# A WKV recurrence on one core: zeros and some thirty steps of the first twelve pairs get other places in the written-out order

## The chip, the cores and the metric

The kernel runs on one core of a Trainium2 chip. The metric is device time in microseconds (us), the median of several executions. The core's engines each work through their own queue in order: PE (TensorE, matmul) with its weight loads, DVE (VectorE), ACT (ScalarE), POOL (GpSimd) and SP (SyncE, which only issues transfers here). They meet through semaphores. Sixteen DMA engines move the data.

## The reference

For each batch and each channel a state (aa, bb) is carried over 2048 time steps, with a running maximum pp for numerical safety. `k` and `v` are 16 x 2048 x 256 in float32, `w` and `u` are vectors of 256.

```python
for t in range(seq_len):
    ww = u + k[b, t];  qq = np.maximum(pp, ww)
    e1, e2 = np.exp(pp - qq), np.exp(ww - qq)
    output[b, t] = (e1 * aa + e2 * v[b, t]) / (e1 * bb + e2 + 1e-08)
    ww = pp - w + k[b, t];  qq = np.maximum(ww, k[b, t])
    e1, e2 = np.exp(ww - qq), np.exp(k[b, t] - qq)
    aa, bb, pp = e1 * aa + e2 * v[b, t], e1 * bb + e2, qq
```

So every output is a ratio of two exponentially weighted sums over the past, with an extra weight `u` on the present step.

## The kernel before

Time is cut into 16 chunks of 128 steps (c = 0 to 15), batches into groups of four, so there are 64 work items, `n` = 0 to 63, which the text calls pairs; chunk c holds pairs 4c to 4c + 3. Each loads 512 KB of `k` and as much of `v`. A program lists the steps of all pairs, gives each a place (a number), sorts them, and emits them in that order as far as their conditions and free buffers allow; each engine then executes its own steps in the order in which they were emitted. The steps that matter here:

- `LK n`, `LV n`: the loads, issued by POOL from pair 3 on (L108, L111, L115). `RK n`: `k` rounded to the matmul type (L194; DVE, or POOL for n = 11, 15, 19 and so on; pairs 3 to 10 are loaded in the rounded type's tile and need none). `CV n`: `v` cast to bf16 (L214; DVE for n under 10, POOL from 10 on).
- `R q n` and `L q n` (q = 0, 1): PE builds the exponents of half q of pair n in an X tile of PSUM (L201, four small matmuls, and L207, two large ones). There are two X tiles. `X q n`: ACT takes the exp of them into the ring EZR (L210), which frees the tile.
- `TV n`: DVE multiplies these weights by `v` (L219). `S n`: PE sums them over time into TOT (L246).
- The state of chunk c, when its four S are done: `CS` (DVE copies the sums, L252), `TU` (PE turns them, L259), `SL` (ACT, logarithm, L263), `FR` and `OF` (DVE, frames by a scan, and offsets, L268 to L276), `SN` (DVE, one value for the next chunk, L279), `SW` (ACT, exp, L282), `CH` (DVE, the chain by two scans, L286 to L289), `SS` (DVE, L296), `KP` (DVE, L299), `TK` (PE turns the result back into the PSUM tile TURN, L303), `BK` (DVE copies TURN out, L307).
- The output of pair n: `DEN n` (PE, twelve matmuls into an X tile, L323), `LN n` and `INV n` (ACT: exp of minus the logarithm gives the reciprocal, L335, L340), `NUM n` (PE, twelve matmuls, L323), `MUL n` (DVE, L355), `ST n` (the stores, SP). Pair n's output comes ten pairs behind its input.

Ahead of some of PE's steps stand zero matmuls (L149): products of a zero tile, written to TURN, that nothing reads. They keep PE at work while it would wait. Their numbers come from the table `Z0` for chunk or pair 0 and `Z` for the rest. From `TK` to `BK` none are emitted, since TURN holds a result then (`quiet`). Places come from the table P; the dictionary `AT` overrides single ones:

```python
key = name if isinstance(name, str) else " ".join(map(str, name))
ops[name] = dict(place=AT.get(key, place), fn=fn, args=args, after=list(after), take=take, give=give, mode=mode)
```

Of the kernel before, what the change touches and what calls it, by code (L numbers as in the profile page):

```python
# [15 lines left out]
def kernel(  # L16
# [37 lines left out]
    FILL = 1  # L54
# [4 lines left out]
         "R": [-0.795, -7.965],  # L59
         "OUT": {"DEN": [-0.47, -0.155, -0.55, -0.495], "LN": [-11.935, -9.86, -0.84, -6.17], "INV": [-13.87, -8.32, -4.99, -5.82], "NUM": [-0.105, 0.155, 0.11, -5.15], "MUL": [1.115, 0.345, 0.895, 1.035], "ST": [-5.05, 7.26, 1.245, 7.765], "SQ": [-3.365, 6.69, -2.4, 8.84]},  # L60
         "TAIL": {"DEN": -4.36, "LN": -16.54, "INV": 3.8, "NUM": -0.31, "MUL": 4.39, "ST": 14.35, "step": 2.989, "SQ": 26.08},
         "Z0": {"L": 1, "S": 3, "DEN": 0, "NUM": 6, "TK": 47, "TU": 17, "R": 12},
         "Z": {"DEN": 0, "L": 1, "NUM": 0, "TK": 4, "S": 0, "TU": 1, "R": 0}}

    AT = {"INV 55": 69.0, "SL 15": 69.1, "LN 56": 69.2, "SW 15": 75.7, "FR 15": 69.3}

    consts = ctx.enter_context(tc.tile_pool(name="consts", bufs=1))
    kpool = ctx.enter_context(tc.tile_pool(name="kpool", bufs=NK))
# [63 lines left out]
    Z = consts.tile([128, 192], BF16, tag="Z", name="Z")  # L132
# [14 lines left out]
    def zeros(m, first=False):  # L147
        for j in range(m):
            K(PE.matmul(TURN[:, 0:192], Z[:, 0:128], Z, start=first, stop=True, skip_group_check=True))  # L149
# [72 lines left out]
    AS, D1, L1, A0, FR, BC, A2 = range(7)  # L222
# [88 lines left out]
    RD, NUM, OT = {}, {}, {}  # L311
# [66 lines left out]
    def step(name, place, fn, args=(), after=(), take=None, give=(), mode=0):  # L378
        key = name if isinstance(name, str) else " ".join(map(str, name))
        ops[name] = dict(place=AT.get(key, place), fn=fn, args=args, after=list(after), take=take, give=give, mode=mode)  # L380

# [51 lines left out]
    while todo:  # L433
        for name in todo:
            o = ops[name]
            if all(x not in ops or "done" in ops[x] for x in o["after"]) and (xs if o["take"] == "X" else free.get(o["take"], 1)):
                break
        else:
            raise AssertionError(todo[:9])
        todo.remove(name)  # L440
        args = list(o["args"])
        if o["take"] == "X":
            held[name] = xs.pop(0)
            args.append(held[name])
        elif o["take"]:
            free[o["take"]] -= 1
        elif name[0] == "L":
            args.append(held[("R",) + name[1:]])
        for g in o["give"]:
            if g == "X":  # L450
                x = held[("DEN", name[1]) if name[0] == "LN" else ("NUM", name[1]) if name[0] == "MUL" else ("R",) + name[1:]]
                xs.append(x)
                args.append(x)
            else:
                free[g] += 1
        if o["mode"] and not quiet:
            zeros(P["Z0" if name[-1] < FILL else "Z"].get(name[0], 0))
        quiet = quiet and name[0] != "BK" or name[0] == "TK"
        o["fn"](*args)
        o["done"] = True  # L460
# [30 lines left out]
```

## Time and profile before

| | |
|---|---|
| Median of three runs | 289.46 us (288.67 to 289.91) |
| The profiled execution | 289.2 us on the device, span 287.5 us |
| Busy in the span | PE 271.6 us (94%, zeros included), ACT 258.6 (90%), DVE 246.9 (86%), POOL 176.4 (61%) |
| Moved | 101.20 MB, 352 GB/s on the mean |
| ACT idle ahead of pair 8's exps | 4.38 us, ended by L207 of PE |
| The zeros ahead of TK 0 | 47, 4.05 us from 29.07 us on |

Times in the profile count from the start of the span; the device time also holds what lies around it. A timeline row gives start and length in us, engine, line of the kernel, operation, output and inputs, how many instructions are merged in the row, and in brackets the idle time of the engine ahead of it and what ended it. A step such as `X 0 8` is not named in the profile: it is the seventeenth instruction of L210.

### The profile page before, as it was taken

What the parts mean: (1) busy time and instruction counts of PE and PEld (TensorE: products, weight loads), DVE (VectorE), ACT (ScalarE), POOL (GpSimd) and SP (SyncE); (2) the same over time, 40 slices, a digit from 0 to 9 for tenths busy, and PEclk for the clock granted to TensorE, in tenths of its full rate; (3) what the DMA queues carried; (4) which work ended last, traced back from release to release, by engine and by line L of the source; (5) the groups of instructions that cost most, each with busy time, mean ns of one, the idle gap of its engine ahead of it and who ended that gap; (6) DMA issues with size and microseconds to landing.
All of it is one profiled execution on the core that took longest, in us unless ns stands there. A gap on an engine that the chain in (4) does not pass through costs nothing.

```text
span 287.5 us, 8058 instructions
## 1 busy us (share of the span) xinstructions
PE 271.6 (94%) x3263; PEld 139.2 (48%) x3263; DVE 246.9 (86%) x422; ACT 258.6 (90%) x291; POOL 176.4 (61%) x219
## 2 busy tenths in 40 slices
PE   7989999999999999999999999999999999998860
PEld 6535744454545545454545545454545545454530
DVE  4685879989897979989898989989898989889861
ACT  1776399999999999999999999999999999998991
POOL 8256458575767687575767687575767685421320
PEclk9999999999999999999999999999999999999997
DMA  6999999999999999999999999999999999985896
GB/s 206 348 354 346 347 348 313 384 369 390 374 394 381 383 393 372 391 382 393 355 392 388 389 387 382 394 385 395 370 380 374 389 394 387 347 237 177 235 278 179
DMA packets 58669, 101.20 MB, mean 352 GB/s; under 512 B 5152, under 2 KB 43688, under 8 KB 58632
## 3 DMA queue, kind: packets, MB, share of 16 engines
q0 software_dynamic: 21200, 65.42, 65.5%
q1 hardware_dynamic: 37280, 35.14, 36.4%
q8 instruction: 25, 0.41, 0.6%
q10 hardware_dynamic: 152, 0.14, 0.1%
q14 instruction: 12, 0.10, 0.1%
HBM read 67.12 MB, written 33.55 MB: 350 GB/s over the span
## 4 chain that ended last, share of the span: by engine, by line
PE 81%; ACT 6%; DMA 4%; DVE 4%; issue 2%; SPq 1%; DVEq 0%; ACTq 0%
PE X L207 20%; PE X L323 15%; PE num L323 12%; PE X L201 12%; PE TURN L149 11%; PE TOT L246 7%; DMA ot<-in_v_dram 4%; ACT rd L335 3%; PE TOT L259 2%; DVE ot L355 2%; ACT rd L340 2%; DVE EZR L219 1%; ACT EZR L210 1%; PE TURN L303 1%; SPq L115 1%
## 5 line engine op out<-in xcount | busy, mean ns | idle before, releaser
L210 ACT ACTIVATE EZR<-X 128x1024 bf16<-128x1024 f32 x128 | 126.9, 1014 | 14.4 <-PE X L207 14.2
L214 POOL CAST vb<-vr 128x1024 bf16<-128x1024 f32 x54 | 56.4, 1044 | 69.3 <-DVE EZR L219 67.5
L219 DVE TENSOR_TENSOR EZR<-EZR,vb 128x2048 bf16<-128x2048 bf16 x64 | 77.8, 1219 | 0.4 <-ACT EZR L210 0.2
L355 DVE TENSOR_TENSOR ot<-num,rd 128x1024 f32<-128x1024 f32 x60 | 73.3, 1221 | 3.9 <-ACT rd L340 3.6
L340 ACT ACTIVATE rd<-rd 128x1024 f32<-128x1024 f32 (+1 forms) x65 | 68.0, 1046 | 2.0
L335 ACT ACTIVATE rd<-X 128x1024 f32<-128x1024 f32 (+1 forms) x65 | 65.8, 1012 | 2.3 <-PE X L323 0.7
L149 PE MATMUL TURN<-Z 128*128 128x192 bf16 x319 | 55.2, 259 | 1.4 <-DVE Z L133 1.4
L201 PE MATMUL X<-WU,CO 64*64 64x512 bf16 x512 | 51.9, 390 | 0.9 <-DVE WU L176 0.6
L149 PEld LDWEIGHTS <-Z 128*128 128x128 bf16 x319 | 28.4, 100 | 48.6 <-issue 47.1
L115 POOL DMA_DIRECT2D vr<-in_v_dram x61 | 46.3, 759 | 6.7 <-DVE vb L214 5.9
L207 PE MATMUL X<-kr,NLE 128*128 128x512 f32 x128 | 45.6, 438 | 0.0
L207 PE MATMUL X<-kr,NLZ 128*128 128x512 f32 x128 | 45.5, 437 | 0.0
L108 POOL DMA_DIRECT2D kf<-in_k_dram x53 | 40.1, 756 | 0.0
L194 DVE CAST kr<-kf 128x1024 fp32r<-128x1024 f32 x39 | 31.6, 839 | 4.0 <-DMA kf<-in_k_dram 4.0
L201 PEld LDWEIGHTS <-CO 64*64 64x64 bf16 x512 | 15.7, 105 | 31.1 <-issue 26.3
L323 PE MATMUL X<-EZR,S 64*64 64x512 bf16 x256 | 26.2, 394 | 1.7 <-ACT rd L335 1.0
L323 PE MATMUL X<-cb,Id 64*64 64x512 bf16 x256 | 25.9, 376 | 0.0
L323 PE MATMUL X<-EZR,Id 64*64 64x512 bf16 x256 | 25.9, 376 | 0.0
L323 PE MATMUL num<-EZR,SN 64*64 64x512 bf16 x240 | 24.3, 386 | 1.1 <-DVE ot L355 1.1
L246 PE MATMUL TOT<-EZR,OH 128*32 128x256 bf16 x512 | 23.7, 277 | 1.3 <-DVE EZR L219 1.3
L323 PE MATMUL num<-cb,IdN 64*64 64x512 bf16 x240 | 24.0, 376 | 0.0
L323 PE MATMUL num<-EZR,IdN 64*64 64x512 bf16 x240 | 23.9, 376 | 0.0
(69 smaller groups left out, 269.3 us busy)
## 6 DMA issues: line engine op xcount, KB each, us to landing
vr<-in_v_dram POOLq DMA_DIRECT2D x61, 512.0 KB, 7.7
kf<-in_k_dram POOLq DMA_DIRECT2D x53, 512.0 KB, 8.5
out_dram<-ot SPq DMA_DIRECT2D x64, 256.0 KB, 10.0
out_dram<-ot SPq DMA_DIRECT2D x116, 128.0 KB, 10.1
kr<-in_k_dram POOLq DMA_DIRECT2D x8, 512.0 KB, 8.8
ot<-in_k_dram SPq DMA_DIRECT2D x3, 512.0 KB, 5.9
ot<-in_v_dram SPq DMA_DIRECT2D x3, 512.0 KB, 10.0
out_dram<-ot POOLq DMA_DIRECT2D x11, 128.0 KB, 3.4
```

Source lines behind the costliest of these rows:

```text
L115: K((SP if n < BYSP else POOL).dma_start(out=vr, in_=rows_of(v, n)))
L149: K(PE.matmul(TURN[:, 0:192], Z[:, 0:128], Z, start=first, stop=True, skip_group_check=True))
L201: K(PE.matmul(X[a][o:o + HS, i, :].rearrange("p (n d) -> p n d", n=2), CO[r:r + HS, q, :], WU[r:r + HS, :].unsqueeze(1).broadcast_to([HS, ...
L207: K(PE.matmul(X[a][:, i, :], (NLE, NLZ)[q], km[:, i, :], start=False, stop=True, skip_group_check=True))
L210: K(SC.activation(ez(n)[:, q, 1], X[a], ACT.Exp))
L214: K((DVE if n < EARLY else POOL).tensor_copy(vb, VR.pop(n)))
L219: K(DVE.tensor_mul(ez(n)[:, :, 0], ez(n)[:, :, 1], vb.unsqueeze(1).broadcast_to([128, 2, 2, D])))
L246: K(PE.matmul(t[32 * j:32 * j + 32, 0:256], OH[:, s:s + 32], ez(n)[:, 0, 1 - q, i, 256 * x:256 * x + 256], start=p == 0 and x == 0, stop=p ...
L323: K(PE.matmul(out_tile[o:o + HS, i, :], left, right, start=s == 0, stop=s == 2, tile_position=(r, o), skip_group_check=True))
L335: K(SC.activation(RD[n][:, i], X[a][:, i], ACT.Ln, scale=RS))
L340: K(SC.activation(RD[n][:, i], RD[n][:, i], ACT.Exp, scale=-1.0))
L355: K(DVE.tensor_mul(o.rearrange("p (i n) d -> p i (n d)", i=2)[:, i], NUM[n][:, i], RD[n][:, i]))
```

## The change

Two things. The numbers of zeros in `Z0` fall (`TK` 47 to 8, `TU` 17 to 2, `R` 12 to 6; the last goes for both halves of pair 0), and a new dictionary `ZAT` puts four zeros each ahead of TU 1, DEN 0 and R 0 11, where none were. And thirty entries of `AT` give steps of pairs 0 to 11 and of the states of chunks 0 and 1 new places.

```diff
-         "Z0": {"L": 1, "S": 3, "DEN": 0, "NUM": 6, "TK": 47, "TU": 17, "R": 12},
+         "Z0": {"L": 1, "S": 3, "DEN": 0, "NUM": 6, "TK": 8, "TU": 2, "R": 6},
...
-    AT = {"INV 55": 69.0, "SL 15": 69.1, "LN 56": 69.2, "SW 15": 75.7, "FR 15": 69.3}
+    AT = {"INV 55": 69.0, "SL 15": 69.1, "LN 56": 69.2, "SW 15": 75.7, "FR 15": 69.3, "TU 0": 5.01, "FR 0": 5.02,
+          "SW 0": 6.2, "TK 0": 7.205, "CV 7": 6.4, "TV 5": 5.1, "S 4": 5.3, "S 5": 7.195, "TV 6": 6.3,
+          "S 6": 7.21, "S 7": 8.1, "CH 0": 6.32, "SS 0": 6.33, "BK 0": 7.21, "CV 6": 5.2, "TV 7": 7.3,
+          "KP 0": 8.6, "TV 8": 8, "R 0 6": 5.0, "R 0 8": 7.19, "R 0 9": 7.9, "CS 1": 8.2, "TU 1": 8.3,
+          "SN 0": 8.15, "FR 1": 8.95, "CV 9": 8.0, "SW 1": 9.6, "RK 11": 9.1}
+
+    ZAT = {"DEN 0": 4, "TU 1": 4, "R 0 11": 4}
...
-            zeros(P["Z0" if name[-1] < FILL else "Z"].get(name[0], 0))
+            zeros(ZAT.get(" ".join(map(str, name)), P["Z0" if name[-1] < FILL else "Z"].get(name[0], 0)))
```

Sorted by these places, with their conditions, the queues come out as follows (zeros in brackets; up to CV 5 on DVE, X 1 5 on ACT and L 1 6 on PE the order is the same, and behind the last step shown too):

```text
PE before   TU 0[17] R 0 7 L 0 7[1] R 1 7 L 1 7[1] TK 0[47] S 4 S 5 R 0 8 L 0 8 R 1 8 L 1 8 S 6
            R 0 9 L 0 9 R 1 9 L 1 9 S 7 R 0 10 L 0 10 R 1 10 L 1 10 TU 1 DEN 0 NUM 0[6]
            R 0 11 L 0 11[1] R 1 11 L 1 11[1]
PE after    TU 0[2] S 4 R 0 7 L 0 7[1] R 1 7 L 1 7[1] R 0 8 L 0 8[1] R 1 8 L 1 8[1] S 5 TK 0[8] S 6
            R 0 9 L 0 9[1] R 1 9 L 1 9[1] S 7 TU 1[4] R 0 10 L 0 10[1] R 1 10 L 1 10[1] DEN 0[4] NUM 0[6]
            R 0 11[4] L 0 11[1] R 1 11 L 1 11[1]
DVE before  CV 6 FR 0 OF 0 CH 0 SS 0 KP 0 TV 5 CV 7 TV 6 TV 7 SN 0 CV 8 TV 8 CV 9 CS 1 BK 0 RK 12 FR 1 OF 1 SN 1
DVE after   FR 0 OF 0 TV 5 CV 6 TV 6 CH 0 SS 0 CV 7 BK 0 TV 7 SN 0 CS 1 KP 0 CV 8 TV 8 CV 9 FR 1 OF 1 SN 1 RK 12
ACT before  X 0 6 X 1 6 SL 0 X 0 7 X 1 7 SW 0 X 0 8 X 1 8 X 0 9 X 1 9 X 0 10 X 1 10 SL 1 LN 0 INV 0 X 0 11 SW 1 X 1 11
ACT after   X 0 6 SL 0 X 1 6 SW 0 X 0 7 X 1 7 X 0 8 X 1 8 X 0 9 X 1 9 SL 1 X 0 10 X 1 10 LN 0 INV 0 SW 1 X 0 11 X 1 11
POOL before CV 10 RK 11          POOL after  RK 11 CV 10          (loads in the same order in both)
```

## The prediction, made before the changed kernel was run

> **What bounds the kernel now.** I read the page first, then busy time by stretch, then the ACT, PE and DVE timelines from 24 to 50 us, and last each load's issue and landing in the trace.
>
> From the page, engine totals, the granted clock and the exps:
>
> ```profile
> PE 271.6 (94%) x3263; PEld 139.2 (48%) x3263; DVE 246.9 (86%) x422; ACT 258.6 (90%) x291; POOL 176.4 (61%) x219
> PEclk9999999999999999999999999999999999999997
> L210 ACT ACTIVATE EZR<-X 128x1024 bf16<-128x1024 f32 x128 | 126.9, 1014 | 14.4 <-PE X L207 14.2
> ```
>
> Busy time by stretch (length; PE, PEld, DVE, ACT, POOL; clock; DMA share; GB/s):
>
> ```profile
> 28.80:36.00 7.20, 7.20 (x89) 5.38 (x87) 6.29 (x14) 2.81 (x5) 2.99 (x4) 1.00 1.34 348
> 36.00:43.00 7.00, 7.00 (x78) 3.44 (x70) 5.38 (x11) 6.34 (x8) 4.03 (x5) 1.00 1.02 348
> 100.00:200.00 100.00, 99.83 (x1222) 49.17 (x1220) 92.50 (x148) 98.51 (x111) 70.20 (x80) 1.00 1.05 385
> ```
>
> PE's high share says little, since zero matmuls fill its waits. ACT works 98.51 of 100 us in the long middle, where four pairs take 16.18 us each time (the first exp of pairs 26, 30, 34 starts at 105.10, 121.28, 137.46). So the middle is bound by ACT, and a change before it counts by how much sooner ACT's unbroken run begins. That is at about 46 us:
>
> ```profile
> 27.23 0.28 ACT L263 ACTIVATE U<-TOT 128x128 f32<-128x128 f32 x1 [0.84 <-PE TOT L259]
> 28.25 2.04 ACT L210 ACTIVATE EZR<-X 128x1024 bf16<-128x1024 f32 x2 [0.74 <-PE X L207]
> 30.19 0.36 ACT L282 ACTIVATE G<-U 128x192 f32<-128x192 f32 x1
> 34.94 2.02 ACT L210 ACTIVATE EZR<-X 128x1024 bf16<-128x1024 f32 x2 [4.38 <-PE X L207]
> ...
> 46.42 1.03 ACT L335 ACTIVATE rd<-X 128x1024 f32<-128x1024 f32 x1 [0.16 <-PE X L323]
> ```
>
> The largest hole is 4.38 us ahead of pair 8's exps, which wait for PE. What PE does there (start, length):
>
> ```profile
> 25.17 1.58 PE L149 MATMUL TURN<-Z 128*128 128x192 bf16 x17
> 26.58 0.61 PE L259 MATMUL TOT<-Sel,ts 128*128 128x96 f32 x4
> ...
> 29.07 4.05 PE L149 MATMUL TURN<-Z 128*128 128x192 bf16 x47
> 32.96 0.39 PE L303 MATMUL TURN<-Id,CB 128*128 128x128 bf16 x4
> 33.28 0.62 PE L246 MATMUL TOT<-EZR,OH 128*32 128x256 bf16 x16
> 33.83 0.41 PE L201 MATMUL X<-WU,CO 64*64 64x512 bf16 x4
> ```
>
> TK 0, with its 47 zeros, stands ahead of pair 8's rows and logs. Loads are the other limit: until 46 us they land one after another every 1.5 us (k8 29.05, k9 32.0, k10 35.1, k11 38.09, v10 39.59, k12 41.13, v11 42.62), as 512 KB at 350 GB/s does. No reordering brings them sooner.
>
> **Zeros at the very start.** R 0 0 and R 1 0 get 6 zeros instead of 12. The first six are hidden: PE waits for WU until 6.83 anyway. The second six (0.08 us each) bring the exps of pairs 0 to 3 some 0.3 to 0.5 us forward, and this ends at v2: it lands at 16.16, CV 2 and then TV 1 (16.86) and S 1 (18.13) wait for it, and R 0 4 stands behind S 1. Worth 0.
>
> **Zeros at TU 0 and SL 0's place.** 15 zeros go, 15 x 0.083 = 1.24 us (the 47 took 3.9 us), so TU 0 starts at 25.34 instead of 26.58 and SL 0 runs from 25.99 (0.65 after TU, as before) to 26.27. SL 0 now stands ahead of X 1 6, which so starts 0.91 us later than before, at 26.27. S 4 comes behind TU 0 (TV 4 ended at 25.80), 0.33 us.
>
> **FR and OF ahead of CV 6, SW 0 ahead of X 0 7.** DVE ends CV 5 at 26.41, the frames and offsets take 1.23 us (28.65 to 29.88), so SW 0 starts at 27.69 and holds ACT for 0.26 us (44.98 to 45.24). X 0 7 follows at 27.95 (before 28.25), X 1 7 at 28.97. The late X 1 6 costs nothing, since ACT waits for SW 0.
>
> **TK 0 behind pair 8.** Steps from the rows of before: exp end to the next rows in its X half 0.20, rows to logs 0.36 to 0.38, logs to the next PE step 0.64, logs to exp 0.75, an exp 1.02. R 0 8 at 29.17, L 0 8 at 29.55 (k8 landed at 29.05), X 0 8 at 30.30 instead of 34.94, 4.64 us sooner; X 1 8 at 31.32. The rest of the walk is where this gain is spent.
> S 5 starts at 31.21 and TK 0's 8 zeros at 31.54 end at 32.20. On DVE, TV 5, CV 6 and TV 6 now stand ahead of CH 0 (1.22 + 0.69 + 1.22 behind 27.64), and CH 0 with SS 0 takes 1.30, to 32.05: the zeros hide this wait, and without them it would be 0.5 us. TK 0 0.40, S 6 0.33, R 0 9 at 32.93. A new wait: the zero ahead of L 0 9 writes TURN, which BK 0 reads. BK 0 stands behind CV 7 on DVE (32.74) and takes 0.68, to 33.42; L 0 9, and all of PE behind it, starts at 33.54, about 0.2 late. X 0 9 at 34.29 (37.27), 2.98 sooner. R 1 9 34.18, L 1 9 34.56, S 7 at 35.20.
> CS 1 ends 1.0 us after S 7's start (38.16 to 39.16 before), at 36.20, and **TU 1**, which now stands ahead of pair 10, waits for it; its 4 zeros lie inside this wait, and R 0 10, both logs of 10 and DEN 0 stand behind it. TU 1 36.24, R 0 10 36.78, L 0 10 37.16, X 0 10 37.91 (39.61), 1.70 sooner. L 1 10 38.18, then DEN 0's 4 zeros, 0.33 us in the open (it also waits for X 0 10's end at 38.93), DEN 0 39.15, LN 0 0.89 later at 40.04 (41.81). NUM 0 with its 6 zeros as before (0.77 + 0.60 + 0.67), then R 0 11's 4 new zeros, 0.33 in the open: R 0 11 at 41.52, X 0 11 at 42.65 (44.06), 1.41 sooner. L 1 11 42.92, S 8 and S 9 at 43.56 (0.55), DEN 1 44.11 (45.53), LN 1 at 45.00 (46.42): 1.42 sooner. From here the order is that of before, and ACT has no holes.
>
> **RK 11, RK 12 and the loads.** RK 11 can start when k11 lands (38.09) and ends at 39.13, not at 41.74; L 0 11 at 41.90 would just be served either way, so this hides under PE. CV 10 then runs at v10's landing, as before, and LK 14, LV 13 and LK 15 go out about 1.1 us sooner, behind a queue that is full to 45.5 us. LV 10 and LK 12, behind the later CV 6, go out 0.5 us later, in a queue of 10 us: nothing. RK 12 now stands behind FR 1, OF 1 and SN 1 and ahead of TV 9. DVE reaches it at 40.4, k12 lands at 41.13, the cast takes 0.7 to 1.14 us, TV 9 ends at 43.1 to 43.5, and S 9 needs it at 43.84: 0.3 us to spare.
>
> **Sum.** 1.4 us, which with roundings of 0.02 to 0.04 us at some ten links is 1.4 to 1.5. In the profiled execution's terms 289.2 - 1.45 = 287.75; its 289.2 lies 0.26 under the median of the runs, so I put the same gain on the median: 289.46 - 1.45 = 288.0. That is 0.5%, about what a measurement of this kernel can tell from no change, so half of this case lies on either side of that bound. The unknown is the price of the 12 new zeros between other steps: nothing (a zero ahead of logs costs 0.02: rows to rows is 1.02 us with it, 1.00 without), or 0.083 each, 1.0 in all. I take the latter, by the 47. Its own range is 287.4 to 288.6.
>
> **Rival: more is kept.** If the zeros cost nothing (1.0 us less) and BK 0 is out of the way (0.2), X 0 9's lead of 2.98 shrinks only to about 2.6: 286.8. For it: PE bubbles hide single zeros. Against: the long rows give 0.083 each. Chance 0.22.
>
> **Rival: the loads take it back.** In the middle k arrives just in time; DVE waits for it at 88, 104 and 185 us:
>
> ```profile
> 88.31 0.70 DVE L194 CAST kr<-kf 128x1024 fp32r<-128x1024 f32 x1 [0.61 <-DMA kf<-in_k_dram]
> 104.56 0.69 DVE L194 CAST kr<-kf 128x1024 fp32r<-128x1024 f32 x1 [0.67 <-DMA kf<-in_k_dram]
> ```
>
> With ACT 1.45 us sooner, loads that can't come sooner hold DVE for that much more each fourth pair; about 0.5 us of it is free (MUL 3 ends at 57.9, NUM 4 follows at 58.4), so some 0.95 of the gain goes: 289.0. Against: the DMA dips to 254 to 340 GB/s from 43 to 50 us and moves 400 at its best against 385 on the mean, so it can catch up before 88 us; and the 0.6 us waits leave ACT's 16.18 us untouched. Chance 0.13.
>
> **Rival on the slow side: PE's rate falls.** 66 zeros go and 18 come (12 by name, 6 ahead of the logs of pairs 8 to 10, which no longer lie between TK 0 and BK 0). Of the first 38, the last 15 took 1.40 us (0.093 each) and the first 23 3.42 (0.149), though the clock column says 1.00: PE starts slow and speeds up after 3.4 us, by 1.6. If PE's waits in the walk (0.3 us at 27.2, 0.7 at 28.5, and 1.2 at 5.6 from the halved zeros of the start) were enough to bring the slow rate back, the stretch from 31.2 to 44.1, in which PE has 12 us of work, would grow by 0.6 for each us so spent. It decides above 4.8 us of such work (2.9 us lost against the forecast); all of it costs 7.2 us. I price it in the middle, 4.5 us lost: 292.5. Against: from 270 to 278 us PE is busy 1.49 of each 2.00 us and the four-matmul groups still follow each other in 0.21 us. Chance 0.10. The Trainium skill, TensorE: Matmul & The Clock Gate, Part 1, says that the clock halves after an idle window of about 3.4 us and returns after a busy one; the start agrees with the 3.4 us, and by that rule waits of 0.7 us keep full rate, but fewer zeros speak against the change as soon as they add up within a window.
>
> That nothing happens is no rival: the list of steps, sorted by the new places, differs on every engine.
>
> **How the numbers follow.** Forecast 0.55, more kept 0.22, loads 0.13, PE's rate 0.10. Faster by over 0.5%: half of the forecast (0.28) and nearly all of the second (0.21), with rounding 0.50. Within: the other half, the loads and a little over, 0.38. Slower: the last, and a worse case of the loads, 0.12. The range runs from 286.6, the second case with 0.2 us to spare, to 289.8, no gain and the spread of the runs.
>
> **What would show it.** Right: X 0 8 at 30.3, X 0 9 at 34.3, X 0 10 at 37.9, LN 1 at 45.0, and from there 1.4 us sooner throughout, to pair 63's exps (254.76 before). Wrong: a hole other than those at 28, 32 to 34 and 37 us; L 0 9 not held by BK 0; RK 12 holding TV 9; DVE waits for k over 1 us after 50 us with ACT holes behind them; matmul groups at more than 0.21 us spacing.

## The result, and the profile after

The changed kernel takes 288.46 us (median of 14 runs, 286.87 to 288.83) beside 289.39 us for the kernel before (14 runs, 288.60 to 290.06). The ratio of the two is 0.995, interval 0.9936 to 0.9964: about 1.45 us at 289.39, between 1.04 and 1.85 by the interval (it compares runs made beside each other; the two medians lie 0.93 apart). The forecast was 288.0 with a gain of 1.45. The profiled execution took 288.83 us with a span of 287.1 (before 289.2 and 287.5). Lines of the changed kernel stand six lower than before: L207 is now L213, L210 is L216, and so on. (The new entries of `AT` are 28, not thirty.)

The page of the changed kernel: totals, the granted clock in 40 slices, and the exps' group.

```profile
PE 268.5 (94%) x3215; PEld 134.8 (47%) x3215; DVE 248.5 (87%) x422; ACT 259.0 (90%) x291; POOL 175.7 (61%) x219
PEclk9999999999999999999999999999999999999996
L216 ACT ACTIVATE EZR<-X 128x1024 bf16<-128x1024 f32 x128 | 126.8, 1014 | 11.5 <-PE X L213 11.5
```

The clock holds in every slice but the last, as before. The exps' waits for PE fell from 14.2 us to 11.5, but the span fell by only 0.4, so not all that the exps won arrived at the end. The ACT timeline of the changed kernel, first the stretch that the change reorders (28 to 47 us), then two lines much later:

```profile
27.64 1.92 ACT L216 ACTIVATE EZR<-X 128x1024 bf16<-128x1024 f32 x2
29.83 2.04 ACT L216 ACTIVATE EZR<-X 128x1024 bf16<-128x1024 f32 x2 [0.27 <-PE X L213]
33.69 2.05 ACT L216 ACTIVATE EZR<-X 128x1024 bf16<-128x1024 f32 x2 [1.82 <-PE X L213]
37.29 2.04 ACT L216 ACTIVATE EZR<-X 128x1024 bf16<-128x1024 f32 x2 [0.74 <-PE X L213]
42.25 2.04 ACT L216 ACTIVATE EZR<-X 128x1024 bf16<-128x1024 f32 x2 [0.43 <-PE X L213]
44.61 1.02 ACT L341 ACTIVATE rd<-X 128x1024 f32<-128x1024 f32 x1 [0.31 <-PE X L329]
...
140.08 1.02 ACT L216 ACTIVATE EZR<-X 128x1024 bf16<-128x1024 f32 x1 [0.35 <-PE X L213]
142.44 1.02 ACT L341 ACTIVATE rd<-X 128x1024 f32<-128x1024 f32 x1 [0.15 <-PE X L329]
```

The single hole of 4.38 us ahead of pair 8 is gone; smaller ones of 0.27, 1.82 and 0.74 us stand ahead of pairs 8, 9 and 10. LN 1 starts at 44.61 where it was 46.42, so the front of the kernel is 1.81 us ahead of the profiled execution of before (part of this is that execution's late start, as shown below). The last two lines are new: ACT, which had no wait for PE there before, now waits at pair 35's exps and once more behind them. The first exp of each pair, in us:

| | before | forecast | after | sooner by |
|---|---|---|---|---|
| X 0 7 | 28.25 | 27.95 | 27.64 | 0.61 |
| X 0 8 | 34.94 | 30.30 | 29.83 | 5.11 |
| X 0 9 | 37.27 | 34.29 | 33.69 | 3.58 |
| X 0 10 | 39.61 | 37.91 | 37.29 | 2.32 |
| X 0 11 | 44.06 | 42.65 | 42.25 | 1.81 |
| LN 1 | 46.42 | 45.00 | 44.61 | 1.81 |
| X 0 12 | 48.44 | | 46.63 | 1.81 |
| pair 36 | | 1.4 sooner | | 1.08 |
| pair 63 | 254.76 | 1.4 sooner | 253.98 | 0.78 |

The lead is 1.81 us at pair 12 and stays so to pair 34. It loses 0.73 at pairs 35 and 36, and 0.33 at pair 56. Another 0.41 goes behind pair 63: the last MUL ends 27.12 us after X 0 63 in both executions, but from there to the end of the span, in which the last stores land, it takes 6.01 us instead of 5.60. That leaves the 0.37 us by which the span fell. PE's timeline of the changed kernel where the spread zeros and the new wait lie:

```profile
31.07 0.83 PE L155 MATMUL TURN<-Z 128*128 128x192 bf16 x8
31.75 0.39 PE L309 MATMUL TURN<-Id,CB 128*128 128x128 bf16 x4
32.06 0.40 PE L252 MATMUL TOT<-EZR,OH 128*32 128x256 bf16 x8
32.40 0.41 PE L207 MATMUL X<-WU,CO 64*64 64x512 bf16 x4
32.91 0.24 PE L155 MATMUL TURN<-Z 128*128 128x192 bf16 x1
32.94 0.71 PE L213 MATMUL X<-kr,NLE 128*128 128x512 f32 x2
```

TK 0's eight zeros, TK 0, S 6, R 0 9, then the single zero ahead of L 0 9. It starts 0.51 us after R 0 9, where such a zero follows its rows by 0.34 to 0.35 elsewhere, because BK 0 reads TURN on DVE until 32.86:

```profile
32.17 0.69 DVE L313 CAST cb<-TURN 128x512 bf16<-128x512 f32 x1 [0.32 <-PE TURN L309]
```

The new wait is where the forecast put it, though BK 0 itself waited 0.32 us for TK 0 and not for CV 7.

Where the lead goes is in three lines of the changed kernel, DVE first, then PE:

```profile
136.13 0.99 DVE L200 CAST kr<-kf 128x1024 fp32r<-128x1024 f32 x1 [1.70 <-DMA kf<-in_k_dram]
137.04 1.21 DVE L361 TENSOR_TENSOR ot<-num,rd 128x1024 f32<-128x1024 f32 x1
138.30 0.41 PE L329 MATMUL num<-EZR,SN 64*64 64x512 bf16 x4 [0.76 <-DVE ot L361]
```

DVE reaches RK 36 early and stands still for 1.70 us until k36 lands at 136.10; in the kernel before it landed at 136.06. A MUL queued behind it starts that much later, the next NUM on PE waits 0.76 us for the tile that MUL frees, and ACT's two holes at 139.7 and 142.3 follow.

### The profile page after: what moved, and what is told of

It is laid out like the page before. It is cut to its first block, busy times and chain, and to the rows that moved or that the text cites. A ratio compares the mean times of both kernels' runs of the same rounds, so it can differ in the third digit from the quotient of the medians.

```text
span 287.1 us, 7961 instructions
## 1 busy us (share of the span) xinstructions
PE 268.5 (94%) x3215; PEld 134.8 (47%) x3215; DVE 248.5 (87%) x422; ACT 259.0 (90%) x291; POOL 175.7 (61%) x219
## 4 chain that ended last, share of the span: by engine, by line
PE 53%; DMA 23%; ACT 10%; DVE 8%; issue 3%; SPq 0%; POOL 0%; DVEq 0%; ACTq 0%; POOLq 0%
DMA out_dram<-ot 19%; PE X L213 14%; PE X L329 10%; PE num L329 8%; PE X L207 8%; PE TURN L155 7%; PE TOT L252 4%; ACT rd L341 4%; ACT EZR L216 3%; DVE ot L361 3%; DMA kr<-in_k_dram 3%; ACT rd L346 2%; DMA WUf<-in_u_dram 2%; DVE EZR L225 2%; PE TOT L265 1%
## 5 line engine op out<-in xcount | busy, mean ns | idle before, releaser
L216 ACT ACTIVATE EZR<-X 128x1024 bf16<-128x1024 f32 x128 | 126.8, 1014 | 11.5 <-PE X L213 11.5
L155 PE MATMUL TURN<-Z 128*128 128x192 bf16 x271 | 53.0, 262 | 1.5 <-DVE Z L139 1.4
L207 PE MATMUL X<-WU,CO 64*64 64x512 bf16 x512 | 51.9, 390 | 1.7 <-DVE WU L182 1.0
L155 PEld LDWEIGHTS <-Z 128*128 128x128 bf16 x271 | 24.5, 101 | 50.6 <-issue 49.1
L213 PE MATMUL X<-kr,NLE 128*128 128x512 f32 x128 | 45.6, 437 | 0.7 <-DMA kr<-in_k_dram 0.7
L213 PE MATMUL X<-kr,NLZ 128*128 128x512 f32 x128 | 45.5, 436 | 0.0
L207 PEld LDWEIGHTS <-CO 64*64 64x64 bf16 x512 | 15.8, 104 | 32.2 <-issue 27.2
```

Of the source, the lines that this page charges most:

```text
L207: K(PE.matmul(X[a][o:o + HS, i, :].rearrange("p (n d) -> p n d", n=2), CO[r:r + HS, q, :], WU[r:r + HS, :].unsqueeze(1).broadcast_to([HS, ...
L213: K(PE.matmul(X[a][:, i, :], (NLE, NLZ)[q], km[:, i, :], start=False, stop=True, skip_group_check=True))
L216: K(SC.activation(ez(n)[:, q, 1], X[a], ACT.Exp))
```

## Experiments

The questions: does the order, or the number of zeros, bring the gain; what do the twelve new zeros cost; does the start matter; and is it the loads that take part of it back? Times are medians; each ratio is to the kernel before, run beside it.

**The zeros alone.** The kernel before, with the three numbers of the change and its old order.

```diff
-"TK": 47, "TU": 17, "R": 12
+"TK": 8, "TU": 2, "R": 6
```

> The order of before with the smaller numbers of zeros (TK 8, TU 2, R 6) and none of the four new places. Theory A (the walk: both the zeros and the order are needed, since DVE and the loads stand behind the zeros): TU 0 1.2 us sooner, but FR 0 stays behind CV 6, which waits for v6; TK 0 starts when SS 0 is done, about 31.7 instead of 32.96; S 5 then waits for TV 5, so pair 8's first exp is 0.3 to 0.6 us sooner (34.4 against 34.94), and RK 12 at k12's landing (41.1) holds FR 1 and TV 9 as before, so LN 1 is at most 0.3 us sooner than 46.42. Time 289.1, ratio 0.998 to 1.000. Rival (the zeros alone are the change, the order adds little): LN 1 1.2 us sooner or more, ratio 0.996 or below.

Measured: 291.05 us, ratio 1.0049 (1.0027 to 1.0071): slower, which neither theory allowed. From its PE timeline, and its busy time by stretch (length; PE, PEld, DVE, ACT, POOL; granted clock; DMA share; GB/s):

```profile
31.45 0.61 PE L303 MATMUL TURN<-Id,CB 128*128 128x128 bf16 x4 [3.22 <-DVE CB L296]
33.80 1.22 PE L207 MATMUL X<-kr,NLE 128*128 128x512 f32 x2
37.54 0.74 PE L207 MATMUL X<-kr,NLE 128*128 128x512 f32 x2
```

```profile
28.30:30.30 2.00, 0.00 (x0) 0.00 (x0) 1.46 (x7) 0.69 (x2) 1.50 (x2) 1.00 1.61 353
30.30:37.10 6.80, 5.65 (x40) 2.17 (x40) 5.95 (x11) 1.35 (x2) 1.95 (x4) 0.50 1.23 350
```

With 8 zeros PE is idle for 3.22 us ahead of TK 0, from 28.23 on, because SS 0 on DVE ends only at 31.39 and all else in PE's queue stands behind TK 0. The granted clock falls to 0.50 at 30.30, 2.07 us into this hole, and stays there until 37.1. In that time the two matmuls of L207 for one half of a pair take 1.22 us, and later 0.74 again. X 0 9 comes at 38.32 (37.27 before), X 0 12 at 49.49 (48.44). So the 47 zeros were not ballast that could all be cut: they held PE's clock over a wait.

**Part of the zeros.** Same edit but `TK` 40.

```diff
-"TK": 47, "TU": 17, "R": 12
+"TK": 40, "TU": 2, "R": 6
```

> The order of before with TK 40, TU 2, R 6: as the run with zeros only, but with 40 instead of 8 zeros ahead of TK 0, so that PE's hole there is 0.8 us instead of 3.2. Theory E (the run with zeros only was slow because the hole of 3.2 us halved PE's rate for some 5 us, 0.53 granted and four-matmul groups at twice the spacing): granted clock 1.00 from 30 to 40 us, logs of pair 8 at 0.7 us and not 1.22, pair 8's first exp at 34.0 to 34.4, pair 12's 0.3 to 0.9 us sooner than 48.44 (part of it by the start's chance), time 288.7 to 289.4, ratio 0.998 to 1.000. Rival (pair 8 behind TK 0 is slow in that order whatever the clock does): 290 or more.

Measured: 289.25 us, ratio 1.0009 (0.9992 to 1.0025): no change. PE's timeline and the stretch:

```profile
31.48 0.40 PE L303 MATMUL TURN<-Id,CB 128*128 128x128 bf16 x4 [0.52 <-DVE CB L296]
33.39 0.73 PE L207 MATMUL X<-kr,NLE 128*128 128x512 f32 x2
```

```profile
30.00:35.00 5.00, 4.07 (x44) 2.11 (x41) 4.77 (x9) 0.94 (x2) 1.63 (x3) 1.00 1.32 346
```

The order, and the time at which TK 0 starts, are the same as in the kernel with 8 (31.48 and 31.45). Only the hole is 0.52 us instead of 3.22, and the clock stays at 1.00 and the logs at 0.73. That shows that the loss in the kernel with 8 is the clock's, not one of the shorter fill itself. It also shows that fewer zeros in the old order win nothing: X 0 8 is at 34.16, and the two kernels below that keep the old order and the old zeros and start early have it at 34.12 and 34.18.

**The order alone.** The changed kernel with the old numbers of zeros and without the twelve new ones.

```diff
-"TK": 8, "TU": 2, "R": 6
+"TK": 47, "TU": 17, "R": 12
...
-ZAT = {"DEN 0": 4, "TU 1": 4, "R 0 11": 4}
+ZAT = {}
```

> The new order with the numbers of zeros of before (TK 47, TU 17, R 12, none in the four new places). Theory A (each zero ahead of TK 0 costs 0.083 us once pair 8 stands ahead of it and DVE's work is done behind it): TK 0 starts some 3.2 us later than in the changed kernel, pair 9's first exp at 37.5 to 38.3 against 33.69 there and 37.27 in before, LN 1 at about 48 to 49, 2 to 2.6 us later than before: 291.5 to 292, ratio 1.007 to 1.009. Rival (zeros only fill waits): LN 1 as in the changed kernel, 44.6, ratio 0.995.

Measured: 291.86 us, ratio 1.0073 (1.0052 to 1.0093). PE's and ACT's timelines:

```profile
32.11 4.05 PE L155 MATMUL TURN<-Z 128*128 128x192 bf16 x47
37.94 2.04 ACT L216 ACTIVATE EZR<-X 128x1024 bf16<-128x1024 f32 x2 [5.04 <-PE X L213]
```

The old 4.05 us of zeros now stand ahead of pair 9, whose exps have a hole of 5.04 us. Pair 8's work fills the wait for SS 0 here, too (its first exp is at 30.86, and SS 0 ends at 32.64), but the zeros come on top of it, so that TK 0 starts at 35.99. Pair 12 is 2.10 us later than before, pair 63 2.50. So neither half is worth anything by itself: with the order alone the zeros fill a wait that pair 8 has already filled, and with the zeros alone nothing fills it.

**Without the twelve new zeros.**

```diff
-ZAT = {"DEN 0": 4, "TU 1": 4, "R 0 11": 4}
+ZAT = {}
```

(One zero stays ahead of TU 1: without an entry in `ZAT` the table `Z` holds.)

> The changed kernel without the four zeros each ahead of TU 1, DEN 0 and R 0 11. Theory A (0.083 us each where PE has no other wait): those ahead of TU 1 lie in the wait for CS 1 and give nothing; those ahead of DEN 0 and R 0 11 give 0.33 us each, less what SW 1 and the loads then hold: LN 1 0.4 to 0.6 us sooner than in the changed kernel (44.0 to 44.2 against 44.61). Rival (single zeros are hidden in PE's pipeline): LN 1 within 0.1 us of 44.61.

Measured: 288.14 us, ratio 0.9952 (0.9929 to 0.9975). TU 1's zeros cost nothing. DEN 0's four cost 0.17 us (DEN 0 starts at 38.38 for 38.55), since it would wait for the release of its X half almost as long. R 0 11's four cost 0.54: from NUM 0's last four matmuls to R 0 11 it takes 0.21 us without them and 0.75 with them. So X 0 11 comes 0.71 us sooner. LN 1, at 44.20, comes only 0.41 sooner, because S 9 now waits on PE (S 8 and S 9 take 0.86 us instead of 0.55) for TV 9, which stands on DVE behind RK 12 and so behind the landing of k12. The lead is 2.22 us at pair 12, yet 1.79 at pair 16, 1.44 at pair 36, 1.50 at pair 63; RK 16 waited 0.79 us for k and RK 36 1.00. The time doesn't tell this kernel from the changed one: what it wins more it gives back.

**Twelve zeros at the start**, in the changed kernel.

```diff
-"TK": 8, "TU": 2, "R": 6
+"TK": 8, "TU": 2, "R": 12
```

> The changed kernel with 12 zeros again ahead of R 0 0 and of R 1 0. Theory A (the start's zeros are worth 0; that v2 landed at 14.6 instead of 16.2 and pair 4's exps came 1.5 us sooner in the changed kernel's profile is chance of the loads and not these zeros): exps of pairs 0 to 3 0.46 us later than in the changed kernel, CV 2 still at v2's landing, LN 1 within 0.1 us of the changed kernel's where v2 lands alike, time within 0.1% of it. Rival (the start's zeros brought the 1.5 us): pair 4's first exp at 19.6 as in before, LN 1 0.3 to 0.5 us later than 44.61.

Measured: 288.14 us, ratio 0.9942 (0.9923 to 0.9961). LN 1 at 44.78, 0.17 later than in the changed kernel; no difference in the time. Pair 4's first exp is at 19.51, where the rival put it, but v2 landed late, at 15.73. With the order alone, which has the same twelve zeros, v2 landed at 14.52 and that exp came at 18.65; with six zeros v2 landed as late as 15.50. So the start goes with the load and not with the zeros. In this execution the lead at pair 12, 1.64 us, was kept to pair 63 (1.65): the loss at pair 36 doesn't come in every execution.

**Room on the DMA.** The kernel before and the changed kernel, each without the two 128 KB stores of pairs 0 to 51, so that this part of the output is never written.

```diff
-for h in range(1 if shared(n) else 2):
+for h in range(1 if shared(n) else 0):
```

> The kernel before without the two 128 KB stores of each of pairs 0 to 51 (a quarter of the written bytes up to there is left out), so that the middle needs 324 GB/s instead of 388. It is the base for the next run. Theory B (the loads, close to the DMA's limit, are what takes part of the changed kernel's lead back; before, they hold DVE at times but cost ACT nothing): its middle is bound by ACT, so pair 63's exps come within 0.3 us of 254.76, and no cast of k waits for its load after 50 us. Rival C (the loads bound the middle of the kernel before as well): 1 us or more faster than before.

> The changed kernel with the same stores left out. Theory B: no cast of k waits after 50 us, the lead at pair 12 (1.6 to 1.8 us against the kernel before) is whole at pair 63 (exps at 253.0 to 253.1 instead of 253.98), and against the run before it in this call the gain is 1.4 to 1.8 us (0.5 to 0.6%). Rival (the lead is lost to something else, in the order of the middle or on ACT): 0.8 to 1.0 us at pair 63, as in the changed kernel's profile.

Measured: 288.89 us (0.9985, 0.9970 to 0.9999) and 287.60 us (0.9936, 0.9914 to 0.9957). DVE's waits for k between 50 and 250 us, first in the kernel before, then in the changed one (sum, count, longest):

```profile
DVE kr L194 <- DMA kf<-in_k_dram: 2.6, 5, 0.7
```

```profile
DVE kr L200 <- DMA kf<-in_k_dram: 4.0, 6, 1.7
```

With fewer stores neither version has such a wait, and the changed one keeps its lead: 1.84 us at pair 12 and 1.84 at pair 63. This fits loads that come just in time as what ate the lead. By itself it is one profile, the run with twelve zeros at the start kept its lead with all stores, and the interval of the time (0.9914 to 0.9957) overlaps that of the changed kernel; the next run decides. The kernel before was expected to keep X 0 63 within 0.3 us of 254.76. It has it at 254.01, since this execution started early (X 0 12 at 47.63 instead of 48.44). Against it the changed kernel is 1.03 us ahead at pair 12 and 1.09 at pair 63, and 1.29 us faster in the medians; 1.4 to 1.8 was expected. The kernel before gains next to nothing by the room, since its waits for k, 0.7 us at the longest, leave ACT without a single wait for PE ahead of exps between 50 and 250 us.

**The rounding of k behind the MUL.** If the loss runs RK, MUL, NUM, ACT, then RK behind the MUL should save it with all loads as they are. In the changed kernel, and by itself in the kernel before, each fourth pair's RK from 16 on goes behind the MUL that follows it:

```diff
-"RK": [-2.85, -1.165, -3.305, -1.485]
+"RK": [-1.9, -1.165, -3.305, -1.485]
...
+"RK 0": -2.85, "RK 12": 9.15
```

> The changed kernel with every fourth pair's rounding of k (pairs 16, 20, 24 and so on) placed behind MUL instead of ahead of it on DVE, where DVE has 0.77 us of idle time ahead of the frames; nothing else on any engine differs. Theory B (the lead is lost where such a rounding waits for its load and MUL, and with it NUM and PE, stands behind it): the lead of pair 12 lasts to pair 63, and the time is 0.2 to 0.7 us under the changed kernel's 288.46, ratio to before 0.992 to 0.994. Rival (DVE's waits don't matter): 288.4, 0.995.

> The kernel before with every fourth pair's rounding of k behind MUL, as in the run that was fastest so far; nothing of the change. Theory B (before, the roundings come when their loads have just landed, so the waits of 0.3 to 0.7 us cost ACT nothing; only a kernel that runs ahead of the loads loses by them): lead at pair 63 as at pair 12, time within 0.2% of before in quiet executions, at most 0.3% faster over all of them (ratio 0.997 to 1.001), so that most of the 0.9% belongs to the two together. Rival D (the later rounding is worth 0.4% or more by itself, whatever comes ahead of it): 0.996 or below.

Measured: 286.78 us, ratio 0.9908 (0.9886 to 0.9931), and 288.38 us, ratio 0.9977 (0.9962 to 0.9991). The first beats both kernels, by more than expected, and its interval lies below that of the changed kernel. Its DVE timeline at the place where the changed kernel lost:

```profile
135.62 1.23 DVE L361 TENSOR_TENSOR ot<-num,rd 128x1024 f32<-128x1024 f32 x1 [1.34 <-ACT rd L346]
136.75 0.69 DVE L200 CAST kr<-kf 128x1024 fp32r<-128x1024 f32 x1
```

MUL runs at 135.62 as soon as ACT's reciprocal is there, 1.42 us earlier than the 137.04 of the changed kernel. RK finds its k landed. The lead is 1.95 us at pair 12 and 2.01 at pair 63. The move does one thing more: RK no longer runs beside a cast on POOL, and takes 0.69 us where it took 0.84 to 1.40 in the changed kernel. That alone does not eat the lead, since in the changed kernel with fewer stores RK still takes 1.37 to 1.41 us and the lead is whole. By itself the move is worth about 0.2%, the change about 0.5%, both together 0.9%; the intervals of the parts leave open whether they merely add up. That only a kernel which runs ahead of the loads loses by such waits, as the second expectation says, is not so: the zeros alone lost 0.36 and 0.35 us more at waits of 0.95 (RK 36) and 1.00 (RK 44), and the order alone 0.34 at a wait of 0.84 (RK 40), and both run later than the kernel before.

**The same without the twelve new zeros.** The edits of the last kernel and of the one without new zeros together.

> The same without the twelve new zeros ahead of TU 1, DEN 0 and R 0 11. Theory B: the 0.3 to 0.5 us that the run without these zeros won at pair 12 and lost again by pair 16 (where a rounding waited 0.79 us for k) is kept: 0.3 to 0.5 us under the run before it, 287.3 to 287.8, ratio 0.990 to 0.993. Rival (the extra lead is lost to the loads in another place, as they come when they come): the same as the run before it.

Measured: 287.02 us, ratio 0.9908 (0.9889 to 0.9928). The lead is 2.29 us at pair 12 and 2.24 at pair 63, so in the profile 0.23 us of what these zeros cost is kept up to pair 63. The time doesn't show it, and in the profile the end of the kernel takes it back: behind the last MUL the span goes on for 6.11 us, against 5.19 in the run before it.

**The changed kernel once more.**

> The changed kernel once more, to see in a second profile where its lead goes. Theory B: lead 1.6 to 1.9 us at pair 12 and, at pair 63, less by what the loads take, at a rounding of every fourth pair where DVE waits over 0.8 us for k; in which pairs is chance. Over the executions 288 to 288.6, ratio 0.994 to 0.997. Rival (the loss is fixed in place, at pairs 36 and 56): the same two places again.

Measured: 288.26 us, ratio 0.9960 (0.9943 to 0.9976). The lead is 1.80 us at pair 12 and 1.45 from pair 36 on, with this line on DVE:

```profile
135.60 1.16 DVE L200 CAST kr<-kf 128x1024 fp32r<-128x1024 f32 x1 [1.15 <-DMA kf<-in_k_dram]
```

The wait is again at RK 36, 1.15 us this time, and nothing is lost at pair 56. Pair 36 is a repeated weak spot (the changed kernel twice, the one without new zeros, and the zeros alone), pair 56 was not.

## Why the prediction was right, point by point

**The walk to LN 1.** Its mechanism held at most links: pair 8's exps run 5.11 us sooner, the gain is spent on TK 0, the wait for BK 0, TU 1 and the new zeros, and what is left at LN 1 stays, up to pair 34. Its times were 0.3 to 0.6 us too late throughout, and 0.31 of that was there at X 0 7 (27.64 for 27.95), before any new zero. Two waits were ended by something else than it said. The frames of chunk 0 waited 0.54 us for SL 0 and not for CV 5; TU 0 came at 24.78 instead of 25.34. And TK 0's eight zeros did not hide 0.5 us of waiting: SS 0 ended at 31.25 instead of 32.05, so the zeros, from 31.07 on, themselves held TK 0 until 31.75, and BK 0 with it. By these rows fewer than eight would do; no run tried it.

**The new zeros.** The forecast calls their price 0.083 us each, 1.0 in all, but its walk counts 0.33 ahead of DEN 0, 0.33 ahead of R 0 11 and nothing ahead of TU 1, together 0.66. The kernel without them bears out the walk's sum: 0.17 and 0.54, and X 0 11 is 0.71 us later with them. Their split was off, and only 0.41 of it is left at LN 1, where TV 9 would have held S 9 otherwise.

**The start's zeros worth 0.** The effect was right (0.17 us at LN 1, nothing in the time), the reason was not. It rested on v2 landing at 16.16, as if that were fixed. It landed at 16.2 in the profile of before, 14.6 in that of the changed kernel, and between 14.05 and 15.73 in the eleven experiments' profiles, with six zeros or twelve. The old order carries a late start on: its X 0 12 is at 48.44 there, and at 47.63 and 47.68 in the two kernels with the old order, the old zeros and an earlier v2. The new order, with the twelve new zeros, comes out at 46.5 to 46.8 from any start. So part of the 1.81 us, up to 0.8, is the start of the one execution of before; against the early starts the front wins about 1.0. A single profile of before could not show that, and how the timed runs started isn't recorded.

**RK 11, RK 12 and TV 9.** DVE cast k12 on landing (41.09 us, forecast 41.13). It reached RK 12 only at 41.00 and not at 40.4, since two small steps ahead of it took three to five times as long as before (last section), and waited 0.09 us. TV 9 ended at 43.02 and S 9's matmuls start at 43.39: the 0.3 us to spare were right, and in the kernel without the new zeros they were used up.

**The loads.** Here the forecast was wrong in its profile though right in its sum. It expected 1.4 us sooner "throughout", and gave 0.13 to the rival that the loads take it back. That rival happened in part, by its own chain (RK waits for k, MUL stands behind, NUM and ACT follow): 0.73 and 0.33 us in the first profile of the changed kernel, 0.35 in the second, none in the one with twelve zeros at the start. One of the forecast's own signs of being wrong was there, too: waits for k of 1.70 and 1.09 us after 50 us, with ACT holes behind them. The kernels with RK behind MUL show the cause. Its place was off: it named each fourth pair, but it bit at pair 36 and once at 56. The step that failed is "it can catch up before 88 us": the loads did keep up there, and were late 50 us further on.

How much of such a wait is free can be read over all profiles: behind 50 us every wait of RK for k up to 0.70 us cost no lead, and every one of 0.79 us or more cost 0.3 to 0.7. The forecast's 0.5 us came from NUM 4 at 58.4, but its first matmul is at 58.24, 0.34 behind the MUL. The rest is free because of POOL. A rounding of the kernel before without a wait:

```profile
71.43 1.40 DVE L194 CAST kr<-kf 128x1024 fp32r<-128x1024 f32 x1
```

The one at 88.31, shown in the prediction, took 0.70 us after a wait of 0.61. A cast on POOL runs beside both, and both end 0.54 to 0.55 us behind the end of that cast (72.29 and 88.47). So a load that lands a little late only shortens the time in which RK would have stood still anyway.

**The sum.** 1.45 us is what the ratio gives, 0.93 what the medians give, and 1.16 the ratio of the second measurement, 0.9960. In the profile it is a front gain larger than forecast, less a loss further on that the sum left out (1.81 - 0.73 - 0.33 = 0.75; 0.78 is read at pair 63, and 0.37 at the end of the span); that the two made up to 1.45 in the time is partly luck.

**More is kept.** It needed zeros that cost nothing and a BK 0 out of the way. The zeros cost 0.71 us at X 0 11 and 0.41 at LN 1, and BK 0 held L 0 9: wrong. It also took 1.0 us off a walk that held only 0.66 for them. A gain of its size in the time came only with the RK move.

**PE's rate falls.** The mechanism is real, as the kernel with the zeros alone shows: in one hole of 3.22 us the clock fell, and the logs went from 0.74 to 1.22 us. It didn't strike the changed kernel, since pair 8's work stands where the 47 zeros stood: PE's waits from 24 to 48 us are 0.48 us at the longest, and the clock stays 9 in all of its slices but the last. The Trainium skill, TensorE: Matmul & The Clock Gate, Part 1, speaks of an idle window of about 3.4 us. The trace differs: here the clock fell after 2.07 us of idleness. That 0.52 us kept it agrees. That small waits add up, the form in which it spoke against this change, no run here shows.

**What the first theory missed.** The expectation for the zeros alone let TK 0 wait for SS 0 and put no price on PE's idleness there. The rival of the prediction already held the answer, at a kernel where it didn't strike.

## What stays open

Why k36 lands late in some executions and not in others: its load was issued at 125.86 us and took 10.24 in the profile of the changed kernel, and with twelve zeros at the start it was issued at 126.04 and took 8.84. What fixes the place wasn't tried. Nor was the end of the kernel: from the last MUL to the end of the span the thirteen profiles take 5.2 to 6.2 us, a spread as large as the front's gain, and no run shows what sets it. TU 0's 15 zeros were never taken out alone, and why four zeros ahead of R 0 11 cost 0.54 us and not 0.33 isn't shown.

## What to carry to other kernels

Filler work that keeps an engine's clock up is worth cutting when real work is moved into its place: in this kernel either half alone made it slower (1.0049 and 1.0073), both made it faster (0.995), and a small part of the filler (TK 47 to 40) could go without any effect. When a change wins time at the front, look for the first operation further on that waits for a load just in time, and for what is queued behind it on its engine; putting that wait behind the work that others need brought the ratio from 0.995 to 0.991. And compare the starts and the ends of the two profiled executions before a difference of under 1 us is read as the change's.

## What the runs showed of the hardware

Some float32 operations on DVE stand still while POOL casts. The changed kernel's DVE lines, then its POOL lines:

```profile
38.30 1.11 DVE L276 TENSOR_TENSOR_SCAN U<-U 128x96 f32<-128x96 f32 x1
39.71 1.06 DVE L281 TENSOR_TENSOR U<-U 128x64 f32<-128x64 f32 x1
```

```profile
38.17 1.04 POOL L200 CAST kr<-kf 128x1024 fp32r<-128x1024 f32 x1 [0.92 <-DMA kf<-in_k_dram]
39.65 1.04 POOL L220 CAST vb<-vr 128x1024 bf16<-128x1024 f32 x1 [0.45 <-DMA vr<-in_v_dram]
```

The scan took 0.36 us in the kernel before and the subtraction 0.22; here both run beside a POOL cast and end 0.20 and 0.08 us after it. The roundings of k on DVE do the same: the 125 of them that start during a POOL cast, in all profiles, end 0.54 to 0.62 us after it, whether they took 0.69 or 1.5 us. RK 11, moved forward, is one of the two casts above. It seems to have cost nothing, as DVE would have waited for k12 until 41.07 anyway, and was not tried by itself. The other surprise was the spread of the first loads: v2's landing lay between 14.05 and 16.16 us in thirteen profiles of twelve kernels that all issue it ahead of anything the edits touch.
